# One weight load for both activation parts: 512-column products in the second layer of a hybrid encoder

## The chip, the cores and the metric

The kernel runs on one core of one Trainium2 chip. The metric is the device time of one execution in microseconds (us). TensorE (PE in the rows) multiplies, and its weight loads have rows of their own (PEld); VectorE is DVE, ScalarE is ACT, GpSimd is POOL, and SP issues most of the DMAs.

## The reference

A trunk of two layers over 272 tokens (16 meta tokens and 256 of the input), 1024 wide, all in float32:

```python
for layer in range(DEPTH):                       # DEPTH = 2
    hn = rms_norm(h, norm_mix[layer])
    proj = hn @ w_in[layer]                      # 1024 -> q, k, v, SSM input, pooling input, 3 x 1024 gates
    y_attn = windowed_gqa_attention(q, k, v, attn_sink[layer])
    y_ssm = bidirectional_s5(...)
    y_pool = multiscale_pool(...)
    ys = jnp.stack([y_attn, y_ssm, y_pool], axis=2)
    branch = jnp.einsum("blcm,cmd->blcd", ys, w_branch[layer])
    gates = jax.nn.sigmoid(proj[..., OFF_GATE:].reshape(b, L, N_BRANCH, D_MODEL))
    merged = jnp.sum(gates * branch, axis=2)
    h = h + merged @ w_out[layer]
    hn = rms_norm(h, norm_mlp[layer])
    h = h + jnp.square(jax.nn.relu(hn @ w_up[layer])) @ w_down[layer]   # 1024 -> 4096 -> 1024
return rms_norm(h, norm_final)[:, N_META:]       # the meta tokens are dropped
```

## The kernel before, in words

Channels lie on the 128 partitions and tokens along the columns. Layer 0 works on all 272 tokens; in layer 1 the meta tokens are needed only for keys, values, SSM and pooling inputs, so that all other products have `N = 256` columns (`t0 = 16` is left out).

**Products in three passes.** Every float32 operand is split in two parts, a high one rounded to `fp32r` and a low one with the remainder, and a product of two 128x128 blocks is made of three `fp32r` matmuls in `product` (line 183): high weights times high activations, high weights times low activations, low weights times high activations. All blocks of one output tile accumulate in one PSUM tile (`mm`, three buffers of one bank). Each matmul has a weight load of its own, so that the high block is loaded twice.

**Weights.** A chunk is eight 128x128 blocks. `need` (line 160) issues its DMA three chunks ahead, and two chunks ahead splits it: ACT writes `hi` (line 169) and DVE writes `lo` (line 170). Both engines run their instructions in the order in which they stand.

**Out of PSUM.** A gate (`gate`, line 1049) is multiplied by the norm's scale on DVE (L1055), and ACT takes a tanh of it. A branch product (`branch`, line 1059) is multiplied by the gate on DVE (L1076, or L1073 in the first branch) and added to `acc` (L1077). A product of the MLP's first matrix (`up`) goes through three ACT instructions (L1166 to L1168) and one of DVE (L1169), one of its second matrix (`dn`) through two of DVE (L1185, L1186). Queries are copied by ACT (L988) for a rotation on PE (`swq`).

**Order.** The main stream of products goes through SSM inputs (`pju`), keys, values, queries (`pjk`, `pjv`, `pjq`), pooling inputs (`pjp`), gates and branches (`pjg`, `br`), the SSM's output gate (`gl`), the merge (`wo`), and twice sixteen `up` chunks and sixteen `dn` chunks. Attention, SSM scans, pooling and the preparation of the SSM's operands are side work: generators that `pump` steps between half chunks of the main stream. A scheduler then orders each engine's instructions.

Of the kernel before, what the change touches and what calls it, by code (L numbers as in the profile page):

```python
# [10 lines left out]
F32 = mybir.dt.float32  # L11
# [7 lines left out]
P = 128  # L19
# [13 lines left out]
# how the side work is woven into the main stream of products: its rate per slot,  # L33
# by generator and layer, and the slots between a step and the product that uses it
# [23 lines left out]
AHEAD = 3  # chunks of weights loaded ahead of their use  # L58
SPLIT = 2  # and split
WARM = 5  # products that warm the tensor engine up  # L60
# [4 lines left out]
# polynomials, highest power first: e^r on +-ln(2)/2, sine and cosine on +-pi/4  # L65
# [5 lines left out]
# columns of the constant table  # L71
# [3 lines left out]
# columns of the SSM operands of eight groups  # L75
# [9 lines left out]
def encoder(ctx: ExitStack, tc: tile.TileContext, a: dict, out: bass.AP):  # L85
# [5 lines left out]
    class TE:  # L91
        """The tensor engine; side work does not overtake what is written before it."""
# [18 lines left out]
    h = cp.tile([P, KT, NT], F32, name="h")  # L111
    xh = cp.tile([P, KT, NT], F32, name="xh")
    xl = cp.tile([P, KT, NT], F32, name="xl")
# [43 lines left out]
    WHOLE = {(0, 0), (0, 2)}  # (layer, branch) multiplied in float32 without a split  # L157
# [21 lines left out]
    def first_need(k):  # L179
        """The first chunks, split one by one."""  # L180
        need(k - SPLIT, pinned=True)

    def product(ps, ws, xs, start=True, stop=True):
        n = len(ws)
        for i, ((wh, wl), (xa, xb)) in enumerate(zip(ws, xs)):
            TE.matmul(ps, _r(wh), _r(xa), start=start and i == 0, stop=False)
            TE.matmul(ps, _r(wh), _r(xb), start=False, stop=False)
            TE.matmul(ps, _r(wl), _r(xa), start=False, stop=stop and i == n - 1)

    ORDER = ((0, 1, 2, 3), (2, 3, 0, 1))  # SSM quarters; the last operands made are still on chip  # L190
# [28 lines left out]
    side = []  # L219

    class Side:
        """Steps of a generator, each yielding its cost and the slots it has to wait after it;
        a slot of the main stream allows it `rate`."""
# [24 lines left out]
    def pump(boost=0.0):  # L248
        """Side work for one slot of the main stream."""
        for e in list(side):  # L250
            e.run(boost or e.rate)
# [20 lines left out]
    def feed(n, k, t0):  # L272
        """Scaled, split copy of h's k-th block, and its squares; the last are returned apart."""
        hk = h[:, k, t0:]
        S.activation(_r(xh[:, k, t0:]), hk, AF.Copy, scale=gain(n, k))
        V.scalar_tensor_tensor(  # L276
            _r(xl[:, k, t0:]), hk, gain(n, k), xh[:, k, t0:], ALU.mult, ALU.subtract
        )
        return squares(k, t0)
# [5 lines left out]
    def stats(name, t0, parts=None):  # L285
        """1/rms of every token, on all partitions; `parts`' squares are still to be summed."""
# [28 lines left out]
    def exp_acc(x):  # L315
        """e^x for x clamped to [-170, 100], to float32's accuracy."""
# [19 lines left out]
    def twice(c, s, co, so, w):  # L336
        """Cosine and sine of twice the angle."""
        V.scalar_tensor_tensor(so, s, 2.0, c, ALU.mult, ALU.mult)
        V.scalar_tensor_tensor(w, s, -2.0, s, ALU.mult, ALU.mult)
        V.tensor_scalar(co, w, 1.0, None, ALU.add)  # L340
# [13 lines left out]
    def ssm_params(l):  # L354
# [4 lines left out]
        m5 = st(5)  # mag^4, mag^3, mag^2, mag, 1  # L359
# [49 lines left out]
        ct, sn = st(4), st(4)  # cosines and sines of 1..4 times the angle  # L409
# [12 lines left out]
        # f = (abar - 1) / lambda  # L422
# [13 lines left out]
        # the factors by half quarter and part: f's real part, and its imaginary part signed  # L436
# [3 lines left out]
        # input side: mag^(3-j) e^(-i (j+1) theta) f, rows in the order  # L440
        # (step, quarter, parity, pair), the steps from the last to the first
# [30 lines left out]
        # powers of abar on the output side  # L472
# [15 lines left out]
    def prepare(l, q, bun):  # L488
        """The SSM operands of the groups 8q..8q+7 of layer l."""
# [16 lines left out]
        # rotations by j times the chunk's angle, and the decay of a chunk  # L506
# [15 lines left out]
        # output matrices: [part, group, power, channel]; power 0 is C itself  # L522
# [17 lines left out]
        # input matrices, rows (parity, channel, step), columns (direction, state),  # L540
        # and between them the response within a chunk
# [69 lines left out]
    def prep(l):  # L611
        """Parameters and operands of layer l's SSM, ahead of the layer that uses them."""
        yield from ssm_params(l)
        for q in range(4):
            while l == 0 and q >= 2 and q - 2 not in scanned:
                yield 0.0, 1
            bun = bundle(f"b{l}{q}")
            yield from prepare(l, q, bun)
            if l == 0 or q >= 2:
                buns[l, q] = bun  # L620
            else:
                for o, e in PIECES:
                    SY.dma_start(bund[q, :, o:e], bun[:, o:e])
# [5 lines left out]
    def scan_quarter(l, q):  # L629
# [22 lines left out]
        # four runs of chunks: real part's halves, imaginary part's halves in reverse  # L652
# [8 lines left out]
        for hb in range(2):  # L661
            # no group crosses the border of a bank
# [18 lines left out]
        # states before each chunk; the chunks run backward on the last 64 partitions  # L681
# [32 lines left out]
        # rotated back, [part, group, chunk], and all chunks put in order  # L714
# [16 lines left out]
        # outputs, rows (parity, step, channel)  # L731
# [23 lines left out]
    cold = []  # quarters whose results are long out  # L755
# [9 lines left out]
    def attention(l, kr, qr, vt, waits):  # L765
# [7 lines left out]
        for gi, (q0, w, mk) in enumerate(groups):  # L773
            yps = pm.tile([P, 512], F32, tag="yps", name=f"yps{l}{gi}", bufs=1)
            n = 4 if w == P else 1
            hw = 2 * w  # columns of two heads
# [103 lines left out]
    with tc.high_priority():  # L880
# [5 lines left out]
        # the tensor engine reaches its full clock while h arrives  # L886
# [38 lines left out]
    for l in range(DEPTH):  # L925
# [3 lines left out]
        xc = [(xh[:, k, t0:], xl[:, k, t0:]) for k in range(KT)]  # L929
        if l == 0:  # L930
            rstd = None

        def scaled(o, ps):
            """Out of PSUM, with the norm's scale if it is still to come."""
# [7 lines left out]
        def proj(i, full=True, name=""):  # L942
            ps = mm_tile(f"pj{name}{l}")
            n = NT if full else N
# [6 lines left out]
        # SSM input  # L951
# [25 lines left out]
        # keys, values, queries  # L977
# [7 lines left out]
        def rope(ps, o, c0, name):  # L985
            n = NT - c0
            xe = tmp(f"xe{name}")[:, :n]
            S.activation(xe, ps, AF.Copy)  # L988
# [26 lines left out]
        def urgent(gen):  # L1015
            """Side work that starts at once, ahead of the rest."""
            e = Side(gen, 5.0, True)
            waits.append(e)
            e.step()
            e.wait += 1  # L1020
            return e
# [9 lines left out]
        # pooling input  # L1031
# [13 lines left out]
        # gates and branches  # L1045
# [3 lines left out]
        def gate(b, m):  # L1049
# [4 lines left out]
            else:  # L1054
                V.tensor_tensor(g, ps, rstd[:, t0:], ALU.mult)  # L1055
# [3 lines left out]
        def branch(b, m2):  # L1059
            ws = need(plans[l, "b", b][m2])  # L1060
            for i in range(2):
                m = 2 * m2 + i
                ps = mm_tile(f"br{l}{b}{m}")[:, :N]
                yy = [tuple(y[:, t0:] for y in ybuf(b, t)) for t in range(4)]
# [7 lines left out]
                if b == 0:  # L1072
                    V.scalar_tensor_tensor(o, g, 1.0, ps, ALU.add, ALU.mult)  # L1073
                else:
                    tb = tmp(f"gb{l}{b}{m}")[:, t0:]
                    V.scalar_tensor_tensor(tb, g, 1.0, ps, ALU.add, ALU.mult)  # L1076
# [32 lines left out]
        zx = [(zs[:, q, t0:], zs[:, 4 + q, t0:]) for q in ORDER[l]]  # L1109
        ys[2] = slots(2, f"ys{l}")  # L1110
        for m2 in range(2):
            gw = need(plans[l, "glu"][m2])
            for i in range(2):
                m = 2 * m2 + i
                ps = mm_tile(f"gl{l}{m}")[:, :N]
# [4 lines left out]
                S.activation(tb, ps, AF.Tanh, scale=0.5, bias=hb)  # L1120
# [12 lines left out]
        mgh, mgl = slots(0, f"mgh{l}"), slots(1, f"mgl{l}")  # L1133
        for m in range(8):
            hi, lo = mgh[:, m, t0:], mgl[:, m, t0:]
            S.activation(_r(hi), acc[:, m, t0:], AF.Copy, scale=0.5)
            V.scalar_tensor_tensor(_r(lo), acc[:, m, t0:], 0.5, hi, ALU.mult, ALU.subtract)
            mg.append((hi, lo))
        for m in range(8):
            ps = mm_tile(f"wo{l}{m}")[:, :N]  # L1140
            product(ps, need(plans[l, "out"][m]), mg)
            V.tensor_tensor(h[:, m, t0:], h[:, m, t0:], ps, ALU.add)
            sq7 = feed(2 * l + 1, m, t0)
        # MLP
# [3 lines left out]
        for f in range(2):  # L1148
            hid = []
            hs = [slots(i, f"hid{l}{f}{i}") for i in range(4)]  # L1150
            for m in range(16):
                ps = mm_tile(f"up{l}{f}{m}")[:, :N]
# [12 lines left out]
                hi, lo = hs[m // 8][:, m % 8, t0:], hs[2 + m // 8][:, m % 8, t0:]  # L1165
                S.activation(re, ps, AF.Relu)  # L1166
                S.activation(sq, re, AF.Square)  # L1167
                S.activation(_r(hi), re, AF.Square)  # L1168
                V.tensor_tensor(_r(lo), sq, hi, ALU.subtract)  # L1169
                hid.append((hi, lo))  # L1170
                pump()
            for m in range(8):
                ps = mm_tile(f"dn{l}{f}{m}")[:, :N]
# [11 lines left out]
                V.tensor_tensor(tb, ps, rq[:, t0:], ALU.mult)  # L1185
# [43 lines left out]
def _pack(w):  # L1229
    """[K, M] in blocks, [M/128, 128, K/128, 128]."""  # L1230
# [4 lines left out]
def _layout(i):  # L1235
# [8 lines left out]
    # SSM channels: as they enter, [quarter, parity, pair, channel], and as they leave  # L1244
    g = np.arange(512).reshape(4, 4, 2, 16)  # quarter, pair, parity, channel
# [33 lines left out]
    lam = np.stack([f["ssm_lam_re"], f["ssm_lam_im"], ld])  # i l d g n  # L1279
    o["lam"] = lam.transpose(1, 2, 4, 0, 3).reshape(L, P, 3, G)  # L1280
    # b: [l, d, g, n, q]
    b = np.stack([f["ssm_b_re"], f["ssm_b_im"]])  # c l d g n q
    b = b.reshape(2, L, 2, 4, 4, 2, 64, 16)  # c l d quarter pair b n q
    o["b_row"] = b.transpose(1, 3, 5, 7, 4, 0, 2, 6).reshape(L, 4, 2, 16, 1024)
    bc = b.reshape(2, L, 2, 4, 2, 4, 64, 16)  # c l d quarter half g n q
    o["b_col"] = bc.transpose(1, 3, 2, 6, 4, 0, 5, 7).reshape(L, 4, P, 256)
    c = np.stack([f["ssm_c_re"], f["ssm_c_im"], f["ssm_c_re"]])
    c = c.reshape(3, L, 2, 4, 8, 16, 64)  # c l d quarter g p n
# [28 lines left out]
```

## Time and profile before

| | |
|---|---|
| time, median of 3 runs | 893.82 us (893.33 to 897.0) |
| span of the profiled execution, first to last instruction | 892.9 us |
| PE busy, PEld busy | 97%, 91% of the span |
| DVE busy, ACT busy | 76%, 61% |

The page gives no time of the profiled execution beside its span of 892.9 us; the median of the runs is 0.9 us above that span. A matmul's busy time reaches from its start to the modelled end of its results, so that it overlaps with the next: what a matmul costs in a dense stream is read from start to start, or as a stretch's length over its count.

### The profile page before, as it was taken

What the parts mean: (1) busy time and instruction counts of PE and PEld (TensorE: products, weight loads), DVE (VectorE), ACT (ScalarE), POOL (GpSimd) and SP (SyncE); (2) the same over time, 40 slices, a digit from 0 to 9 for tenths busy, and PEclk for the clock granted to TensorE, in tenths of its full rate; (3) what the DMA queues carried; (4) which work ended last, traced back from release to release, by engine and by line L of the source; (5) the groups of instructions that cost most, each with busy time, mean ns of one, the idle gap of its engine ahead of it and who ended that gap; (6) DMA issues with size and microseconds to landing.
All of it is one profiled execution on the core that took longest, in us unless ns stands there. A gap on an engine that the chain in (4) does not pass through costs nothing.

```text
span 892.9 us, 18412 instructions
## 1 busy us (share of the span) xinstructions
PE 870.0 (97%) x7174; PEld 814.8 (91%) x7174; DVE 675.3 (76%) x1443; ACT 541.0 (61%) x1005; POOL 4.1 (0%) x32
## 2 busy tenths in 40 slices
PE   6999999999999999999999999999999999999995
PEld 4987777899899999999999988789999999999995
DVE  7987978899986557677896988677878755555564
ACT  5568597845567655477565467575565775357652
POOL 1000000000000000000000000000000000000000
PEclk7999999999999999999999999999999999999998
DMA  7644645454475556958766464625565565555551
GB/s 250 203 154 129 191 117 164 151 159 152 154 228 170 177 169 194 294 187 264 230 201 182 130 215 150 206 96 157 174 192 170 175 193 182 186 185 186 189 189 48
DMA packets 62520, 159.47 MB, mean 179 GB/s; under 512 B 20064, under 2 KB 25952, under 8 KB 62432
## 3 DMA queue, kind: packets, MB, share of 16 engines
q1 hardware_dynamic: 59696, 155.63, 55.8%
q10 hardware_dynamic: 2736, 2.65, 0.9%
q8 instruction: 56, 0.92, 0.4%
q14 instruction: 32, 0.26, 0.1%
HBM read 150.79 MB, written 7.47 MB: 177 GB/s over the span
## 4 chain that ended last, share of the span: by engine, by line
PE 79%; DVE 12%; ACT 4%; DMA 3%; issue 2%; DVEq 0%; ACTq 0%; SPq 0%
PE up L96 21%; PE dn L96 21%; PE pjg L96 10%; PE br L96 5%; PE wo L96 5%; DVE lo L170 3%; PE pju L96 3%; PE s L96 2%; PE pjp L96 2%; PE yps L96 1%; PE pt L101 1%; PE pjq L96 1%; PE l L96 1%; PE tp L96 1%; ACT hi L169 1%
## 5 line engine op out<-in xcount | busy, mean ns | idle before, releaser
L170 DVE TENSOR_TENSOR lo<-raw,hi 128x1024 fp32r<-128x1024 f32 x240 | 292.8, 1221 | 131.4 <-ACT hi L169 128.6
L169 ACT ACTIVATE hi<-raw 128x1024 fp32r<-128x1024 f32 x240 | 253.8, 1058 | 227.6 <-PE dn L96 75.2
L96 PE MATMUL dn<-hid,hi 128*128 128x272 f32 (+1 forms) x1024 | 188.0, 285 | 0.0
L96 PEld LDWEIGHTS dn<-hid,hi 128*128 128x128 f32 x1024 | 159.1, 188 | 0.1
L96 PE MATMUL up<-xh,hi 128*128 128x272 f32 (+1 forms) x512 | 146.2, 286 | 0.0
L96 PE MATMUL dn<-hid,lo 128*128 128x272 f32 (+1 forms) x512 | 146.1, 285 | 0.0
L96 PE MATMUL up<-xh,lo 128*128 128x272 f32 (+1 forms) x512 | 146.0, 285 | 0.0
L96 PE MATMUL up<-xl,hi 128*128 128x272 f32 (+1 forms) x512 | 145.9, 285 | 0.0
L96 PE MATMUL pjg<-xh,hi 128*128 128x272 f32 (+1 forms) x384 | 113.8, 296 | 0.0
L96 PE MATMUL pjg<-xh,lo 128*128 128x272 f32 (+1 forms) x384 | 111.2, 290 | 0.0
L96 PE MATMUL pjg<-xl,hi 128*128 128x272 f32 (+1 forms) x384 | 111.0, 289 | 0.0
L96 PEld LDWEIGHTS up<-xl,hi 128*128 128x128 f32 x512 | 96.3, 188 | 0.5 <-DVE xl L276 0.4
L96 PEld LDWEIGHTS up<-xh,hi 128*128 128x128 f32 x512 | 96.5, 189 | 0.3
L96 PEld LDWEIGHTS up<-xh,lo 128*128 128x128 f32 x512 | 96.6, 189 | 0.0
L96 PEld LDWEIGHTS dn<-hid,lo 128*128 128x128 f32 x512 | 96.5, 188 | 0.0
L96 PEld LDWEIGHTS pjg<-xh,hi 128*128 128x128 f32 x384 | 73.0, 190 | 4.9 <-issue 3.9
L96 PEld LDWEIGHTS pjg<-xh,lo 128*128 128x128 f32 x384 | 73.1, 190 | 2.1 <-issue 2.0
L96 PEld LDWEIGHTS pjg<-xl,hi 128*128 128x128 f32 x384 | 72.9, 190 | 1.8 <-issue 1.5
L96 PE MATMUL wo<-mgh,hi 128*128 128x272 f32 (+1 forms) x128 | 36.6, 287 | 0.6 <-ACT hi L169 0.6
L96 PE MATMUL wo<-mgh,lo 128*128 128x272 f32 (+1 forms) x128 | 36.2, 285 | 0.3 <-DVE lo L170 0.3
L96 PE MATMUL wo<-mgl,hi 128*128 128x272 f32 (+1 forms) x128 | 36.2, 285 | 0.1
L1167 ACT ACTIVATE rs<-re 128x272 f32<-128x272 f32 (+1 forms) x64 | 27.1, 424 | 1.8
(351 smaller groups left out, 1635.9 us busy)
## 6 DMA issues: line engine op xcount, KB each, us to landing
raw<-in_w_in_dram SPq DMA_DIRECT2D x76, 512.0 KB, 3.5
raw<-in_w_up_dram SPq DMA_DIRECT2D x64, 512.0 KB, 4.2
raw<-in_w_dn_dram SPq DMA_DIRECT2D x64, 512.0 KB, 4.0
raw<-in_w_br_dram SPq DMA_DIRECT2D x24, 512.0 KB, 4.0
raw<-in_w_out_dram SPq DMA_DIRECT2D x16, 512.0 KB, 3.7
b<-in_b_row_dram SPq DMA_DIRECT2D x16, 256.0 KB, 5.0
b<-ffd SPq DMA_DIRECT2D x16, 256.0 KB, 4.6
raw<-in_glu_w_dram SPq DMA_DIRECT2D x4, 512.0 KB, 4.3
```

Source lines behind the costliest of these rows:

```text
L96: i = nc.tensor.matmul(*args, **kw)
L101: i = nc.tensor.transpose(*args, **kw)
L169: S.activation(_r(hi), raws[j], AF.Copy)
L170: i_ = V.tensor_sub(_r(lo), raws[j], hi)
L1167: S.activation(sq, re, AF.Square)
```

## The change

In layer 1 the two parts of the activations are laid side by side: `xh` and `xl` become two halves of one tile `xx`, and the tiles of the branches' inputs, the merge and the MLP's hidden layer hold the high part of block m at place m and its low part at place m + 4, so that `both` can address the two as one operand of 2 x 256 columns. `product` then issues two matmuls for a block: high weights times both parts (512 columns, one weight load), and low weights times the high part (256 columns), which adds to the second half of the PSUM tile. `total` adds the halves on the way out: ACT copies the second half to SBUF, DVE adds the first. Layer 0, whose two parts have 544 columns, keeps its three matmuls.

```diff
-    xh = cp.tile([P, KT, NT], F32, name="xh")
-    xl = cp.tile([P, KT, NT], F32, name="xl")
+    xx = cp.tile([P, KT, 2, NT], F32, name="xx")
+    xh, xl = xx[:, :, 0], xx[:, :, 1]
...
+    def both(ap, i, t0):
+        return ap[:, i : i + 5 : 4, t0:]
...
     def product(ps, ws, xs, start=True, stop=True):
         n = len(ws)
+        if isinstance(xs[0], bass.AP):
+            c = ps.shape[1] // 2
+            for i, ((wh, wl), x) in enumerate(zip(ws, xs)):
+                TE.matmul(ps, _r(wh), _r(x), start=start and i == 0, stop=False)
+                TE.matmul(ps[:, c:], _r(wl), _r(x[:, 0]), start=False, stop=stop and i == n - 1)
+            return
...
+        side_by = 2 * N <= 512
+        xc = [xx[:, k, :, t0:] if side_by else (xh[:, k, t0:], xl[:, k, t0:]) for k in range(KT)]
+        W_ = 2 * N if side_by else N
...
+        def total(o, ps):
+            if not side_by:
+                return ps
+            S.activation(o, ps[:, N:], AF.Copy)
+            V.tensor_tensor(o, o, ps[:, :N], ALU.add)
+            return o
...
-            S.activation(xe, ps, AF.Copy)
+            if ps.shape[1] == n:
+                S.activation(xe, ps, AF.Copy)
+            else:
+                ps = total(xe, ps)
...
-                V.tensor_tensor(g, ps, rstd[:, t0:], ALU.mult)
+                V.tensor_tensor(g, total(g, ps), rstd[:, t0:], ALU.mult)
...
-                    V.scalar_tensor_tensor(o, g, 1.0, ps, ALU.add, ALU.mult)
+                    V.scalar_tensor_tensor(o, g, 1.0, total(o, ps), ALU.add, ALU.mult)
...
-                    V.scalar_tensor_tensor(tb, g, 1.0, ps, ALU.add, ALU.mult)
+                    V.scalar_tensor_tensor(tb, g, 1.0, total(tb, ps), ALU.add, ALU.mult)
...
-                S.activation(tb, ps, AF.Tanh, scale=0.5, bias=hb)
+                S.activation(tb, total(tb, ps), AF.Tanh, scale=0.5, bias=hb)
...
-            V.tensor_tensor(h[:, m, t0:], h[:, m, t0:], ps, ALU.add)
+            for c in range(0, W_, N):
+                V.tensor_tensor(h[:, m, t0:], h[:, m, t0:], ps[:, c : c + N], ALU.add)
...
-                S.activation(re, ps, AF.Relu)
-                S.activation(sq, re, AF.Square)
-                S.activation(_r(hi), re, AF.Square)
+                if side_by:
+                    total(re, ps)
+                    V.scalar_tensor_tensor(sq, re, 0.0, re, ALU.max, ALU.mult)
+                    S.activation(_r(hi), sq, AF.Copy)
+                else:
+                    S.activation(re, ps, AF.Relu)
+                    S.activation(sq, re, AF.Square)
+                    S.activation(_r(hi), re, AF.Square)
...
-                V.tensor_tensor(tb, ps, rq[:, t0:], ALU.mult)
+                V.tensor_tensor(tb, total(tb, ps), rq[:, t0:], ALU.mult)
```

On PE, at the norm's sum of squares (`ss_f`) in layer 1's first MLP half, a block of `up` stood in three rows before (`xh` and `xl` are the parts, `hi` and `lo` the weights):

```order
L96 MATMUL up_8995<-xh,hi_8919 128x256
L96 MATMUL up_8995<-xl,hi_8919 128x256
L96 MATMUL up_8995<-xh,lo_8920 128x256
L96 MATMUL ss_f_9026<-ssq,consts 128x256
L96 MATMUL ss_f_9026<-sq_8950,consts 128x256
L96 MATMUL up_9044<-xh,hi_8961 128x256
L96 MATMUL up_9044<-xl,hi_8961 128x256
L96 MATMUL up_9044<-xh,lo_8962 128x256
```

and now stands in two:

```order
L96 MATMUL up_8703<-xx,hi_8641 128x512
L96 MATMUL up_8703<-xx,lo_8642 128x256
L96 MATMUL ss_f_8726<-ssq,consts 128x256
L96 MATMUL ss_f_8726<-sq_8665,consts 128x256
L96 MATMUL up_8745<-xx,hi_8676 128x512
L96 MATMUL up_8745<-xx,lo_8677 128x256
```

The place is the same, and each block has lost one matmul with its load. So it goes for 114 chunks of layer 1, which are 912 blocks: 32 `up`, 32 `dn`, 24 gates, 12 branch, 8 `wo`, 4 query and 2 `gl` chunks. The 10 chunks of layer 1 with 272 columns and all of layer 0 keep their matmuls.

On DVE, in the last branch of layer 1 (`br` is its PSUM tile, `gb` the gated product, `lo` a chunk's low weights), one chunk took these rows before:

```order
L1076 SCALAR_TENSOR_TENSOR gb_8546<-gates_6855,br_8533 128x256
L1076 SCALAR_TENSOR_TENSOR gb_8562<-gates_6855,br_8549 128x256
L1077 TENSOR_TENSOR acc_6856<-acc_6856,gb_8546 128x256
L1077 TENSOR_TENSOR acc_6856<-acc_6856,gb_8562 128x256
L170 TENSOR_TENSOR lo_8568<-raw_8527,hi_8567 128x1024
```

and takes these now (L952 is the addition in `total`, L1104 and L1105 are the old L1076 and L1077):

```order
L952 TENSOR_TENSOR gb_8359<-gb_8359,br_8350 128x256
L952 TENSOR_TENSOR gb_8373<-gb_8373,br_8364 128x256
L1104 SCALAR_TENSOR_TENSOR gb_8359<-gates_6826,gb_8359 128x256
L1104 SCALAR_TENSOR_TENSOR gb_8373<-gates_6826,gb_8373 128x256
L1105 TENSOR_TENSOR acc_6827<-acc_6827,gb_8359 128x256
L1105 TENSOR_TENSOR acc_6827<-acc_6827,gb_8373 128x256
L170 TENSOR_TENSOR lo_8381<-raw_8344,hi_8380 128x1024
```

Two additions have come in ahead of the products that they feed, and the next low weights stand behind all six.

On ACT, among the last gates of layer 1, nothing read the PSUM tile of a gate before; now each gate and each branch product has a copy (L951) in ACT's row, between the splits of the weights (L169), the tanh (L1081) and the SSM's GELU (L761, whose input `yq` comes by DMA):

```order
L951 ACTIVATE gates_6826<-pjg_8047 128x256
L761 ACTIVATE zt<-yq_1_8007 128x272
L1118 ACTIVATE zs_7443<-zt 128x256
L169 ACTIVATE hi_8103<-raw_8075 128x1024
L1081 ACTIVATE gates_6826<-gates_6826 128x256
L951 ACTIVATE gates_6826<-pjg_8074 128x256
L951 ACTIVATE gb_8116<-br_8107 128x256
```

The row of the second copy stands behind the GELU and a split. Over the whole program DVE has 144 instructions more (each output tile that changed has one more, a tile of `up` two), ACT 36 more, and PE 912 matmuls fewer.

## Rows read from the trace of the kernel before

**Rows 1.** The page: span, and busy time of each engine.

```profile
span 892.9 us, 18412 instructions
PE 870.0 (97%) x7174; PEld 814.8 (91%) x7174; DVE 675.3 (76%) x1443; ACT 541.0 (61%) x1005; POOL 4.1 (0%) x32
```

**Rows 2.** The chain that ended last: start us, length us, what it was.

```profile
279.93 42.36 PE up L96 x336
...
528.02 0.44 PE pt L101 x4
...
705.43 0.86 PE ss_f L96 x4
...
746.04 45.44 PE dn L96 x384
791.48 45.44 PE up L96 x384
...
882.41 0.44 DVE db L1185
```

**Rows 3.** Busy time by stretch of layer 1, and the granted clock.

```profile
core 0: us, PE busy (x) PEld busy (x) DVE busy (x) ACT busy (x) POOL busy (x), PEclk, DMA share, GB/s
530.00:560.00 30.00, 30.00 (x222) 24.28 (x219) 26.37 (x63) 20.73 (x39) 0.00 (x0) 1.00 0.45 150
560.00:600.00 40.00, 38.93 (x326) 32.44 (x325) 28.72 (x72) 25.59 (x54) 0.00 (x0) 0.96 0.45 147
600.00:640.00 40.00, 40.00 (x415) 38.42 (x414) 32.93 (x61) 23.45 (x35) 0.00 (x0) 1.00 0.52 158
640.00:677.00 37.00, 36.20 (x292) 34.99 (x292) 28.26 (x51) 21.56 (x38) 0.00 (x0) 1.00 0.61 193
746.00:882.00 136.00, 136.00 (x1152) 136.00 (x1151) 76.92 (x99) 71.08 (x111) 0.00 (x0) 1.00 0.54 171
```

**Rows 4.** Two weight loads after a pause of PE, in order of time.

```profile
702.21 0.19 PEld L96 LDWEIGHTS up<-xl,hi 128*128 128x128 f32 x1 [0.23 <-DVE xl L276]
702.32 0.19 PEld L96 LDWEIGHTS up<-xh,lo 128*128 128x128 f32 x1
```

**Rows 5.** Matmuls after which PE empties before the next load, in order of time.

```profile
530.56 0.28 PE L96 MATMUL pjg<-xh,lo 128*128 128x256 f32 x1
530.77 0.20 PEld L96 LDWEIGHTS yps<-pts,vt 128*64 128x64 f32 x4
...
539.92 0.59 PE L96 MATMUL pps<-dl,raw 128*128 128x256 f32 x2
540.44 0.29 PEld L96 LDWEIGHTS s<-qk 64*128 64x128 f32 x2 [0.33 <-issue]
```

**Rows 6.** Groups (460 to 880 us): busy us, mean ns, idle before and releasers.

```profile
L169 ACT ACTIVATE hi<-raw 128x1024 fp32r<-128x1024 f32 x126 | 133.2, 1058 | 131.4 <-PE dn L96 42.8 <-PE up L96 23.0 <-issue 17.7
...
L1055 DVE TENSOR_TENSOR gates<-pjg,rstd_m 128x256 f32<-128x256 f32 x24 | 10.0, 417 | 6.4 <-PE pjg L96 6.3
...
L988 ACT ACTIVATE xeq<-pjq 128x256 f32<-128x256 f32 x4 | 1.4, 361 | 0.0
...
L749 ACT ACT_TABLE_LOAD x3 | 3.8, 1283 | 3.6 <-DMA yq<-yd 3.6
```

**Rows 7.** The chain in layer 1's last branch.

```profile
669.06 1.14 DVE lo L170
670.19 0.66 DVE gb L1076 x2
...
673.99 1.14 DVE lo L170
```

More of the change, by code (lines that the diff above doesn't have):

```diff
@@ L928, in encoder @@
         xs = [(xh[:, k, :], xl[:, k, :]) for k in range(KT)]
-        xc = [(xh[:, k, t0:], xl[:, k, t0:]) for k in range(KT)]
+        side_by = 2 * N <= 512
+        xc = [xx[:, k, :, t0:] if side_by else (xh[:, k, t0:], xl[:, k, t0:]) for k in range(KT)]
+        W_ = 2 * N if side_by else N
         if l == 0:
             rstd = None
+        def total(o, ps):
[4 more added lines that the diff above has]
+            return o
         def scaled(o, ps):
@@ L943, in proj @@
             ps = mm_tile(f"pj{name}{l}")
-            n = NT if full else N
+            n = NT if full else W_
             ws, x_ = need(i), xs if full else xc
@@ L1062, in branch @@
                 m = 2 * m2 + i
-                ps = mm_tile(f"br{l}{b}{m}")[:, :N]
-                yy = [tuple(y[:, t0:] for y in ybuf(b, t)) for t in range(4)]
+                ps = mm_tile(f"br{l}{b}{m}")[:, :W_]
+                yy = [
+                    both(ys[b], t, t0) if side_by else tuple(y[:, t0:] for y in ybuf(b, t))
+                    for t in range(4)
+                ]
                 if (l, b) in WHOLE:
@@ L1108, in encoder @@
         cold.clear()
-        zx = [(zs[:, q, t0:], zs[:, 4 + q, t0:]) for q in ORDER[l]]
+        zx = [
+            both(zs, q, t0) if side_by else (zs[:, q, t0:], zs[:, 4 + q, t0:]) for q in ORDER[l]
+        ]
         ys[2] = slots(2, f"ys{l}")
@@ L1114, in encoder @@
                 m = 2 * m2 + i
-                ps = mm_tile(f"gl{l}{m}")[:, :N]
+                ps = mm_tile(f"gl{l}{m}")[:, :W_]
                 product(ps, [gw[4 * i + q] for q in ORDER[l]], zx)
@@ L1132, in encoder @@
         mg = []
-        mgh, mgl = slots(0, f"mgh{l}"), slots(1, f"mgl{l}")
+        mgs = [slots(i, f"mg{l}{i}") for i in range(2)]
         for m in range(8):
-            hi, lo = mgh[:, m, t0:], mgl[:, m, t0:]
+            b_ = mgs[m // 4]
+            hi, lo = b_[:, m % 4, t0:], b_[:, 4 + m % 4, t0:]
             S.activation(_r(hi), acc[:, m, t0:], AF.Copy, scale=0.5)
             V.scalar_tensor_tensor(_r(lo), acc[:, m, t0:], 0.5, hi, ALU.mult, ALU.subtract)
-            mg.append((hi, lo))
+            mg.append(both(b_, m % 4, t0) if side_by else (hi, lo))
         for m in range(8):
-            ps = mm_tile(f"wo{l}{m}")[:, :N]
+            ps = mm_tile(f"wo{l}{m}")[:, :W_]
             product(ps, need(plans[l, "out"][m]), mg)
-            V.tensor_tensor(h[:, m, t0:], h[:, m, t0:], ps, ALU.add)
+            for c in range(0, W_, N):
+                V.tensor_tensor(h[:, m, t0:], h[:, m, t0:], ps[:, c : c + N], ALU.add)
             sq7 = feed(2 * l + 1, m, t0)
@@ L1151, in encoder @@
             for m in range(16):
-                ps = mm_tile(f"up{l}{f}{m}")[:, :N]
+                ps = mm_tile(f"up{l}{f}{m}")[:, :W_]
                 ws = need(plans[l, "up", f][m])
@@ L1164, in encoder @@
                 sq = tmp(f"rs{l}{f}{m}")[:, t0:]
-                hi, lo = hs[m // 8][:, m % 8, t0:], hs[2 + m // 8][:, m % 8, t0:]
-                S.activation(re, ps, AF.Relu)
-                S.activation(sq, re, AF.Square)
-                S.activation(_r(hi), re, AF.Square)
+                b_ = hs[m // 4]
+                hi, lo = b_[:, m % 4, t0:], b_[:, 4 + m % 4, t0:]
+                if side_by:
[6 more added lines that the diff above has]
+                    S.activation(_r(hi), re, AF.Square)
                 V.tensor_tensor(_r(lo), sq, hi, ALU.subtract)
-                hid.append((hi, lo))
+                hid.append(both(b_, m % 4, t0) if side_by else (hi, lo))
                 pump()
             for m in range(8):
-                ps = mm_tile(f"dn{l}{f}{m}")[:, :N]
+                ps = mm_tile(f"dn{l}{f}{m}")[:, :W_]
                 for q in range(2):
```

## The prediction

> **What bounds the kernel now.** I read the page first, then the chain, then the stretches of layer 1. PE and its weight loads are busy nearly the whole span, DVE three quarters of it [rows 1]; the busy share of PE says little, since overlapping matmuls fill it, so the chain has to say where PE decides. In the MLP it does alone: 384 matmuls follow each other in 45.44 us with nothing between them [rows 2], 0.1183 us each, and in the same stretch DVE is busy 57% and ACT 52% [rows 3]. Layer 0's are 42.36 / 336 = 0.1261 us [rows 2], with 272 columns instead of 256.
>
> Before the merge it is otherwise. From 530 to 677 us DVE is busy 116.3 of 147 us [rows 3], and in the last branch the chain runs on DVE alone: from one `lo` at 669.06 to the second next at 673.99 are two chunks, 2.47 us each [rows 7].
>
> **What a 512-column matmul costs.** This is the term on which the sign hangs, and the trace has no such row. The question is what the 0.1183 us are made of. [...]
>
> [...] A load with no matmul beside it gives way to the next one after 0.11 us [rows 4], and the transposes, each with a load of 128 columns, follow each other in 0.44 / 4 = 0.110 us [rows 2]; so a load alone doesn't set 0.118. Second, where PE has to empty before the next load, a stream can be timed without a load beside it: the float32 passes of `pps` are 0.215 us each (as those of `ss_f`, 0.86 / 4 [rows 2], half the column rate at the full clock), and the next load starts 0.52 us after the first of two, which is 0.09 after the second one's stream; after the `fp32r` matmul it starts 0.21 us after its start [rows 5], so that its stream took 0.21 - 0.09 = 0.12 us, to some 0.01, with no load running beside its end. [...]
>
> [...]
>
> [...] A block then takes 0.235 + 0.118 = 0.353 us instead of 0.355. Where PE sets the pace, in 64 chunks of `up` and `dn` and 8 of `wo`, that is 576 blocks: **-1.1 us** (-12.7 to +3 by the bounds). The loads saved themselves cost nothing now, because they lie beside the streams.
>
> **What is added, and where it lies.** A copy of a 128x256 tile out of PSUM takes ACT 0.36 us (L988), an operation of DVE on one 0.42 alone [rows 6] and 0.33 in a row, two in 0.66 [rows 7].
>
> - *MLP, inside:* 16 + 32 additions of `up` and `dn` come on DVE between 746 and 882 us, 16 of them in `dn` and two in each of 16 `up` tiles; 48 x 0.42 = 20 us on 76.9 of 136 [rows 3] leave DVE idle 39 us. Nothing, and ACT loses work there. Were this cover gone, it would cost those 20 us.
> - *Tail:* the last `dn` tile's way out is on the chain (the DVE row at 882.41 [rows 2]). Copy and addition come before it: 0.36 + 0.42 = **+0.8**.
> - *Last branch:* DVE sets the pace with 2.47 us a chunk; two additions make it 3.13, which is over the 8 x 0.353 = 2.82 us of PE. Eight additions: 8 x 0.33 = **+2.6**. The split of the next low weights stands behind them, and PE waits for that.
> - *Output gate of the SSM (`gl`):* its results go through ACT and DVE in turn before the last branch can start; one copy and one addition more on that way, **+0.8**.
> - *Gates and the first two branches:* 24 + 16 tiles, 40 additions, 13.2 us of DVE in a stretch where it has some 30 us idle in all [rows 3]. Both ends are possible: 0 if the idle time takes them, 13.2 if each stands in the way. ACT's row is new as a place to wait, too: its split of 1.06 us and the GELU, before whose table loads ACT stood still 3.6 us in all for a DMA [rows 6], now stand ahead of copies, and what is queued behind a late copy is DVE's addition, then DVE's next `lo`, then PE. Three PSUM buffers cover two chunks of that. As DVE is already busy 79% with work that comes in bursts, I take nearly a third of the upper end: **+4**. The 256 blocks here save 0.5 us by the price above, which this estimate includes.
> - *Queries:* the addition comes before the rotation for which PE waits, four times some 0.25: **+1**.
> - *Merge:* a second addition to `h` before the last part of `xx` that `up` needs: **+0.4**. Otherwise DVE's chunk of `wo` stays under PE's.
>
> The copies of ACT in `dn` and `wo` lie beside PE. SP's DMAs are the same; three pairs among them change places in the scan stretch, with nothing on the chain behind them.
>
> The sum is -1.1 + 0.8 + 2.6 + 0.8 + 4 + 1 + 0.4 = +8.5 us on the span of 892.9, 901.4; the runs' median lies 0.9 above that span, so 902 us.
>
> **Rivals.** *The load is the cost after all (faster).* If the 512 columns stream in 0.215 us beside their load, and the 256 stay at 0.118, a block takes 0.333: 576 x 0.022 = -12.7 us, and with the same costs of 9.6 the time is 891. If the 256-column matmul also falls to the 0.110 of the transposes, it takes 0.325: -17.3 us, 886, and with part of the 256 blocks of the gate stretch, less. Below 889.3 (0.5% faster) it comes when the two matmuls of a block take less than 0.3305 us together. For it speaks that loads are busy in the same rhythm as matmuls, so a trace can't wholly part the two; against it rows 5 and the two layers' difference. [...]
>
> [...]
>
> *DVE takes the additions in its idle time.* Without the terms for gates, `gl` and queries, 902.3 - 5.8 = 896.5: no change. Its 30 us of idle time speak for it; that they come in front of the very rows that wait for PE speaks against.
>
> *The way out becomes the bound.* With all 13.2 us of the gate stretch on the path, 902.3 + 9.2 = 911.5.
>
> **How the numbers follow.** The forecast (columns cost the same, the gate stretch pays in part) has 0.50; the load as the cost 0.17, at 887 as the middle of its two forms; a part of it 0.10; DVE's idle time 0.15; the way out as bound 0.08. A change of 0.5%, 4.5 us, is about what a measurement of this kernel can tell from none, and the limits are 889.3 and 898.3. Faster is nearly all of the first rival and a little of the second, 0.18; the same, the rest of these two and the third, 0.25; slower, 0.57. The forecast's own range is 898 to 906. For 8 in 10 the range has to take in the upper half of the first rival and to stop short of the last: 887 to 908.
>
> **What would show it.** Right: `up` and `dn` stretches of some 45.2 us (256 matmuls in each, a 512-column start to the next start 0.235 us); 3.1 us between the `lo` rows of the last branch; DVE and not PE on the chain from 640 to 677; the same layer 0. Wrong: MLP stretches of 42.6 us or less, which is the first rival; or DVE with idle time left in the gate stretch and no more of it on the chain. A pause of PE at the step from `up` to `dn`, where the last hidden tile now goes ACT, DVE, DVE, ACT, DVE, would add a cost that I have put at nothing.

## The result and the profile after

The changed kernel takes 906.2 to 909.5 us, 1.0158 times the kernel before (95% interval 1.0127 to 1.0189): some 15 us slower, where +8.5 had been forecast, and just over 908 us, the upper end of the stated range. The first profiled execution, at a mean granted clock of 0.71, took 1493.0 us and is left out, so the rows below are from the same kernel run again (`again`: median 908.71 us against 892.75, ratio 1.0174, 1.0159 to 1.0190).

The page, which answers to [rows 1]:

```profile
span 906.8 us, 16758 instructions
PE 870.9 (96%) x6262; PEld 771.5 (85%) x6262; DVE 726.6 (80%) x1587; ACT 548.0 (60%) x1041; POOL 4.1 (0%) x32
```

PE has lost 912 matmuls and is busy as long; DVE has 51 us more. The chain of the changed kernel, which answers to [rows 2, 7] (start us, length us, what):

```profile
592.84 5.49 PE pjg L96 x16
...
638.89 7.41 PE pjg L96 x32
...
651.21 5.60 PE pjg L96 x32
...
679.31 1.14 DVE lo L170
...
682.78 1.14 DVE lo L170
...
686.26 1.13 DVE lo L170
...
760.02 45.15 PE dn L96 x256
805.17 44.80 PE up L96 x256
...
895.22 0.39 ACT db L951
...
895.63 0.43 DVE db L952
```

The MLP does what was forecast: 45.15 and 44.80 us for 128 blocks each, 0.353 and 0.350 us a block. The two new rows of the tail are 0.39 and 0.43 us. But three groups of gate matmuls are uneven: 16 blocks take 5.60 us at 651, the same 16 take 7.41 at 639, and 8 take 5.49 at 593, twice what they need. Busy time by stretch, which answers to [rows 3], and one short stretch in it (us, busy of PE, PEld, DVE, ACT and POOL, granted clock, DMA share, GB/s):

```profile
530.00:560.00 30.00, 29.55 (x167) 21.02 (x164) 26.91 (x68) 22.15 (x46) 0.00 (x0) 1.00 0.45 151
560.00:600.00 40.00, 36.10 (x242) 27.38 (x241) 32.41 (x84) 27.11 (x60) 0.00 (x0) 0.91 0.48 160
600.00:640.00 40.00, 38.10 (x275) 31.25 (x274) 31.79 (x64) 25.66 (x46) 0.00 (x0) 0.99 0.44 139
640.00:677.00 37.00, 34.40 (x222) 29.14 (x222) 30.86 (x58) 23.34 (x48) 0.00 (x0) 0.96 0.56 176
746.00:882.00 136.00, 136.00 (x776) 118.66 (x775) 100.03 (x159) 71.21 (x116) 0.00 (x0) 1.00 0.57 187
...
592.00:598.00 6.00, 5.16 (x16) 4.39 (x17) 5.19 (x12) 3.10 (x8) 0.00 (x0) 0.50 0.28 87
```

From 592 to 598 the granted clock is 0.50, right after a pause of PE of 3.90 us. The waits of PE from 490 to 720 us (us in total, times, longest):

```profile
PE pjg L96 <- DVE gates L952: 5.8, 2, 3.9
PE wo L96 <- ACT mg L1167: 3.6, 1, 3.6
PE br L96 <- DVE ys L1157: 2.6, 2, 1.8
```

In the kernel before, the longest wait in this place was 0.9 us, and the merge (`wo`) started at 675.3:

```profile
PE yps L96 <- ACT pts L833: 0.9, 1, 0.9
```

```profile
675.28 0.68 PE L96 MATMUL wo<-mgh,hi 128*128 128x256 f32 x2
```

So the whole loss lies ahead of the MLP: the merge starts 14.6 us later than before (689.9 against 675.3), and from there to the end it is 0.7 us less.

What happens in the longest pause is seen in the timelines of PE, ACT and DVE (start us, us, engine, line, what; in brackets the idle time before and what ended it):

```profile
585.87 0.28 PE L96 MATMUL pjg<-xx,lo 128*128 128x256 f32 x1
...
588.65 0.28 PE L96 MATMUL br<-yp,lo 128*128 128x256 f32 x1
592.84 0.79 PE L96 MATMUL pjg<-xx,hi 128*128 128x512 f32 x1 [3.90 <-DVE gates L952]
...
586.07 1.06 ACT L169 ACTIVATE hi<-raw 128x1024 fp32r<-128x1024 f32 x1 [2.71 <-PE pjg L96]
587.14 1.28 ACT L819 ACT_TABLE_LOAD   x1
...
590.07 0.51 ACT L821 ACTIVATE p<-p,sc 128x272 f32<-128x272 f32 x1
590.48 0.19 ACT L821 ACTIVATION_READ_ACCUMULATOR p<-p,sc 128x1 f32 x1
590.57 0.36 ACT L951 ACTIVATE gates<-pjg 128x256 f32<-128x256 f32 x1
...
590.32 0.72 DVE L737 TENSOR_TENSOR x<-z,b10s 128x544 f32<-128x544 f32 x1
...
592.39 0.39 DVE L952 TENSOR_TENSOR gates<-gates,pjg 128x256 f32<-128x256 f32 x1
```

The last gate product is done at 586.15. Its copy (L951) stands in ACT's queue behind a weight split, a table load and the softmax (L821), and runs at 590.57; its addition (L952) stands in DVE's queue behind rows of the SSM scan (L737) and runs at 592.39. Until then the PSUM tile is taken, all three are full, and PE waits.

### The profile page after: what moved, and what is told of

Its sections match the earlier page's. It is cut to its first block, busy times and chain, and to the rows that moved or that the text cites. A ratio compares the mean times of both kernels' runs of the same rounds, so it can differ in the third digit from the quotient of the medians.

```text
span 1491.2 us, 16758 instructions
## 1 busy us (share of the span) xinstructions
PE 1468.4 (98%) x6262; PEld 1187.6 (80%) x6262; DVE 736.8 (49%) x1587; ACT 550.6 (37%) x1041; POOL 4.1 (0%) x32
## 4 chain that ended last, share of the span: by engine, by line
PE 98%; DVE 1%; ACT 1%; issue 0%; POOL 0%; DVEq 0%; ACTq 0%; POOLq 0%
PE up L96 21%; PE dn L96 20%; PE pjg L96 17%; PE br L96 9%; PE wo L96 6%; PE pjp L96 3%; PE pju L96 3%; PE pjq L96 3%; PE s L96 2%; PE l L96 2%; PE yps L96 2%; PE y L96 2%; PE pt L101 2%; PE gl L96 1%; PE tp L96 1%; PE pjv L96 1%
## 5 line engine op out<-in xcount | busy, mean ns | idle before, releaser
L169 ACT ACTIVATE hi<-raw 128x1024 fp32r<-128x1024 f32 x240 | 253.5, 1057 | 605.7 <-PE up L96 155.1
L96 PE MATMUL up<-xx,hi 128*128 128x272 f32 (+1 forms) x768 | 296.0, 461 | 0.0
L96 PE MATMUL dn<-hid,hi 128*128 128x272 f32 (+1 forms) x768 | 291.8, 455 | 0.0
L96 PE MATMUL pjg<-xx,hi 128*128 128x272 f32 (+1 forms) x576 | 246.3, 500 | 2.0 <-DVE gates L952 2.0
L96 PEld LDWEIGHTS up<-xx,hi 128*128 128x128 f32 x768 | 169.5, 234 | 44.1 <-issue 21.6
L96 PE MATMUL up<-xx,lo 128*128 128x272 f32 (+1 forms) x512 | 200.9, 392 | 0.0
L96 PEld LDWEIGHTS pjg<-xx,hi 128*128 128x128 f32 x576 | 151.4, 286 | 41.0 <-issue 22.6
L96 PE MATMUL pjg<-xx,lo 128*128 128x272 f32 (+1 forms) x384 | 163.7, 426 | 0.0
L96 PEld LDWEIGHTS up<-xx,lo 128*128 128x128 f32 x512 | 119.8, 234 | 3.0 <-issue 0.2
L96 PEld LDWEIGHTS pjg<-xx,lo 128*128 128x128 f32 x384 | 106.0, 276 | 5.9 <-issue 4.0
L96 PE MATMUL wo<-mg,hi 128*128 128x272 f32 (+1 forms) x192 | 80.8, 499 | 3.5 <-ACT mg L1167 3.5
```

Source lines behind the costliest of these rows:

```text
L96: i = nc.tensor.matmul(*args, **kw)
L169: S.activation(_r(hi), raws[j], AF.Copy)
```

## The experiments

Each time is set against runs of the kernel before on the same chip. "Over none" is the difference to the kernel before plus the 4.2 us by which `no_total` is under it, that is, the price of a way out over having none. Such a price carries the intervals of two comparisons, together some 2 us.

**The changed kernel again** (no edit).

> The changed kernel itself once more, for a profile at the full granted clock. The forecast's theory (the 512 columns cost what two matmuls of 256 cost, and the way out costs the rest): up and dn stretches of layer 1 of about 45.2 us each, as 256 matmuls in 128 blocks of 0.353 us, and the whole loss of 12 to 15 us ahead of the MLP, between 490 and 700 us of the span, with DVE or ACT on the chain of waits there. The rival that the 512-column matmul itself is dearer (0.242 us or more): up and dn stretches of 46 us or more. The rival that the load is the cost: 43 us or less, and then over 20 us lost ahead of the MLP.

It took 16.0 us more than before, a little over the 12 to 15 expected; the MLP stretches and the place of the loss are as the forecast's theory has them.

**Three matmuls again, in the new tiles.**

```diff
-                TE.matmul(ps, _r(wh), _r(x), start=start and i == 0, stop=False)
+                TE.matmul(ps[:, :c], _r(wh), _r(x[:, 0]), start=start and i == 0, stop=False)
+                TE.matmul(ps[:, c:], _r(wh), _r(x[:, 1]), start=False, stop=False)
```

> The changed kernel's tiles and its way out, but each block again in three matmuls of 256 columns, two of them with the high weights loaded apart, into the two halves of the PSUM tile. What differs from the changed kernel is the 512-column matmul alone. The forecast's theory (the way out costs, the matmul gives 0.002 us a block): about 910 us, within 3 us of the changed kernel. The rival that the 512-column matmul is what costs: back to 895 to 900 us. The rival that the load saved gives time back: 915 us or more.

907.09 us, +14.3, ratio 1.0162 (1.0145 to 1.0179): within 2 us of the changed kernel. The 512-column matmul isn't the loss.

**Two matmuls, the way out of before.** The merge's second addition and the new rows of `up` are gone too.

```diff
-            S.activation(o, ps[:, N:], AF.Copy)
-            V.tensor_tensor(o, o, ps[:, :N], ALU.add)
-            return o
+            return ps[:, :N]
...
```

> The changed kernel's two matmuls to a block, but the way out of the kernel before: results are read from the first half of the PSUM tile alone, with no copy and no second addition, so that the low-part products of layer 1 are left out of the result. The forecast's theory: the way out is gone, and the time is that of the kernel before less the 1 us of the matmuls, 891 to 895 us. The rival that the 512-column matmul is dearer: 898 us or more. The rival that the load saved gives time: 886 us or less.

888.52 us, -4.2, ratio 0.9952 (0.9937 to 0.9966). It lies between the two theories: the matmuls give more than the 1 to 2 us forecast. Its stretch with the first pause has a clock of 1.00, where the kernel before had 0.96 [rows 3] and the changed one 0.91:

```profile
560.00:600.00 40.00, 39.92 (x280) 29.50 (x281) 29.29 (x73) 28.79 (x58) 0.00 (x0) 1.00 0.50 160
```

**Matmuls by themselves.** A kernel of runs of 64 matmuls (128 for float32) with one tile name each.

> Matmuls alone; the whole computation is left out. Runs of 64 fp32r matmuls into PSUM, each with a load of 128 columns, with 64, 128, 192, 256, 272, 320, 384, 448 and 512 columns; 256 and 512 columns also with loads of 64 and of 32 columns; float32 with 128 and 256; 256 columns once more at the end. Spacing from start to start. The forecast's theory: time goes with the columns, 0.118 us at 256 (whatever the load), 0.126 at 272, 0.235 at 512. [...] The third case, that each column further costs what 256 to 272 cost: 0.242 at 512.

Its chain (`nd` 256 columns, `ne` 272, `nh` 448, `ni` 512, each with a load of 128 columns; `mpu` 256 and `mqu` 512 with a load of 64; `fl` 256 in float32, `back` as `nd`):

```profile
56.39 7.69 PE nd L106 x64
64.09 8.02 PE ne L106 x64
...
92.61 13.22 PE nh L106 x64
105.83 14.55 PE ni L106 x64
120.38 7.26 PE mpu L106 x64
...
134.89 14.71 PE mqu L106 x64
...
178.72 27.63 PE fl L106 x128
...
222.00 7.69 PE back L106 x64
```

By 64: 0.120 us at 256, 0.125 at 272, 0.207 at 448, 0.227 at 512. So 512 columns cost 1.89 times 256, less than the 0.235 forecast and more than the 0.215 of the first rival. With a load of 64 columns, 256 cost 0.113: 0.007 us hang on the load. At 512 nothing does (0.230). A float32 pass of 256 columns takes 27.63 / 128 = 0.216, which is 1.80 times the 0.120 of `fp32r`, where the forecast has half the column rate. It is one execution, with a mean granted clock of 0.949 over its 232.8 us; the 256 columns at the end take the same 7.69 us as the first.

**The additions of one stretch alone.** Relative to the kernel without them (`added` is the two-instruction way out):

```diff
...
# gates_total: gates and first two branches
-                V.tensor_tensor(g, total(g, ps), rstd[:, t0:], ALU.mult)
+                V.tensor_tensor(g, added(g, ps), rstd[:, t0:], ALU.mult)
...
-                    V.scalar_tensor_tensor(tb, g, 1.0, total(tb, ps), ALU.add, ALU.mult)
+                    V.scalar_tensor_tensor(tb, g, 1.0, (added if b < 2 else total)(tb, ps), ALU.add, ALU.mult)
...
# last_total: last branch
+                    V.scalar_tensor_tensor(tb, g, 1.0, (added if b == 2 else total)(tb, ps), ALU.add, ALU.mult)
```

> Two matmuls to a block everywhere, but the halves are added only for the gates and the first two branches; everywhere else the result is read from the first half alone, so that there the low-part products of layer 1 are left out. The forecast put this stretch at 4 us. The theory after the first runs is that this stretch is the mis-sized term, with some 10 us: the run without any addition, 888.5 us, plus 10, that is 897 to 900 us. The forecast's size: 892 to 893 us. If the loss comes only from additions everywhere together: 890 us.

901.06 us, +7.8 (ratio 1.0078, 1.0052 to 1.0103): **12.0 us over none**.

> Two matmuls to a block everywhere, but the halves are added only in the last branch; everywhere else the result is read from the first half alone, so that there the low-part products of layer 1 are left out. The forecast put this at 2.6 us, so 891 us over the 888.5 of the run without additions. The theory after the first runs is a loss of 4 to 5 us, as DVE is late there and TensorE then pauses and goes on at the lower clock: 892 to 894 us. If that pause comes from the gate stretch before it: 889 us.

893.55 us, +0.2 (ratio 0.9993, 0.9979 to 1.0007): **4.5 us over none**. Its longest wait of PE, two rows of DVE's timeline in the branch, and the stretch behind it:

```profile
PE wo L96 <- ACT mg L1170: 3.6, 1, 3.6
```

```profile
668.18 1.22 DVE L170 TENSOR_TENSOR lo<-raw,hi 128x1024 fp32r<-128x1024 f32 x1
...
671.65 1.22 DVE L170 TENSOR_TENSOR lo<-raw,hi 128x1024 fp32r<-128x1024 f32 x1
```

```profile
676.00:680.00 4.00, 4.00 (x15) 3.42 (x14) 2.71 (x7) 0.14 (x1) 0.00 (x0) 0.57 0.12 16
```

DVE works from 663.1 to 678.7 with hardly a gap; from `lo` to `lo` it needs 3.47 us here, for a split and seven operations, one of them left over from the tile before. PE waits 3.6 us for the merge's input and then has a clock of 0.57 for 4 us: (1 - 0.57) x 4 = 1.7 us, an estimate, on top of the 2.6 for eight additions.

**Halves of the way out.** Relative to the changed kernel; `copy_only` also leaves out the merge's second addition, which `add_only` keeps:

```diff
# copy_only
-            S.activation(o, ps[:, N:], AF.Copy)
-            V.tensor_tensor(o, o, ps[:, :N], ALU.add)
+            S.activation(o, ps[:, :N], AF.Copy)
...
# add_only
-            S.activation(o, ps[:, N:], AF.Copy)
-            V.tensor_tensor(o, o, ps[:, :N], ALU.add)
+            V.tensor_tensor(o, consts[:, :N], ps[:, :N], ALU.add)
```

> Half of the way out: ACT copies the first half out of PSUM, DVE adds nothing, so that the low-part products of layer 1 are left out. Theory A, the cost is DVE's time: 889 to 892 us, near the run without a way out (888.5). Theory B, the cost is that every result first waits in ACT's queue: 900 us or more. If both count: 894 to 898 us.

> The other half of the way out: DVE adds a constant table to the first half, ACT copies nothing; the second half of the products of layer 1 is left out but for the merge, and the constant changes the result. Theory A, the cost is DVE's time: 903 to 908 us, near the changed kernel (908.7). Theory B, the cost is ACT's queue: 893 us or less. If both count: 897 to 901 us.

Copy alone: 892.01 us, -1.3, so 2.9 over none. Addition alone: 896.47 us, +3.2 (ratio 1.0026, 1.0010 to 1.0043), 7.4 over none. Theory A fits the first run and not the second, and theory B fits neither. Together the halves should make 10.3, and the changed kernel has 20.2. Some 10 us belong to the pair.

**What the pair does.** Four kernels, relative to the changed one:

```diff
# act_both: t is a tile of 512 columns
...
+            S.activation(t, ps, AF.Copy)
+            V.tensor_tensor(o, t[:, N:], t[:, :N], ALU.add)
# both_apart: nobody reads spare
...
+            S.activation(spare, ps[:, N:], AF.Copy)
+            V.tensor_tensor(o, consts[:, :N], ps[:, :N], ALU.add)
# copy_then_add
+            S.activation(o, ps[:, :N], AF.Copy)
+            V.tensor_tensor(o, o, consts[:, :N], ALU.add)
# add_then_copy: for gates and branches o is a tile of its own
...
+            V.tensor_tensor(o, consts[:, :N], ps[:, :N], ALU.add)
+            S.activation(spare, o, AF.Copy)
```

> The changed kernel, but ACT copies both halves (512 columns, one instruction) into SBUF, and DVE adds them there. DVE's and TensorE's work is the same, ACT's is more by some 0.3 us a tile; a PSUM tile is free when ACT has passed. Theory H (the tile is held until two engines have come by one after the other): faster than the changed kernel, 900 us or less. Theory T (the time of the two engines together fills the stretch): 908 us or more, since ACT has more to do. Theory Q (DVE stands still behind ACT's copies): no better either, 906 us or more, since DVE waits for ACT as before.

905.59 us, +12.3, 16.5 over none: 3.7 less than the changed kernel although ACT has more to do: it is busy 127.5 of the 175 us from 530 to 705, in the changed kernel 114.8. A part of the cost may be the held tile, but less than theory H had.

> ACT copies the second half into a tile that nobody reads, and DVE adds a constant table to the first half, so that the second half of the products of layer 1 is left out but for the merge, and the constant changes the result. Both engines have the changed kernel's instructions, and both must pass before a PSUM tile is free, but DVE never waits for ACT. Theory T (engine time): 906 us or more, as the changed kernel. Theory Q (DVE's wait for ACT's copy): 899 us or less, near the run with the addition alone (896.5). Theory H (the tile is held until both have come by): in between, 899 to 905 us, since the two come by in either order, but the later one still counts.

909.30 us, +16.0, 20.2 over none, the same as the changed kernel. By its expectation theory T would be right and Q fallen; but its waits of DVE (520 to 700 us) show that the edit did not do what it was for:

```profile
DVE gb L955 <- ACT spare L954: 2.7, 1, 2.7
...
DVE gates L955 <- ACT spare L954: 2.2, 4, 1.0
```

DVE still waits for ACT's copy, five times and 4.9 us in all, though it reads nothing of it; what the two have in common is the PSUM tile. So this run decides nothing about Q.

> ACT copies the first half into SBUF, and DVE adds a constant table to the copy, so that the second half of the products of layer 1 is left out but for the merge, and the constant changes the result. ACT's and DVE's instructions are as many and as long as in the changed kernel, and DVE waits for ACT's copy as there; but a PSUM tile is free as soon as ACT alone has passed. Theory H (a tile held until two engines have passed is what makes 20 us out of 3.5 and 8): 900 us or less, near the sum of the two halves of the way out, 888.5 + 3.5 + 8. Theory T (the two engines' time): 906 us or more. In between, 901 to 905 us: the hold is a part of it.

905.74 us, +12.0, 16.2 over none: 4.0 less, between what the two theories expect and near T's end. A tile that ACT alone sets free is worth some 4 us; DVE still waits for ACT, and 6 us over the two halves' 10.3 remain.

> DVE adds a constant table to the first half, and ACT then copies the sum into a tile that nobody reads, so that the second half of the products of layer 1 is left out but for the merge, and the constant changes the result. ACT's and DVE's instructions are as many and as long as in the changed kernel, but DVE alone sets a PSUM tile free, and for gates and branches DVE never waits for ACT's copy. Theory T (the two engines' time alone): 905 us or more. Theory Q (what costs is that DVE, and with it the PSUM tile, waits for its turn in ACT's queue): 900 us or less, near the addition alone (896.5) and the copy's 3.

899.17 us, +5.0 (ratio 1.0060, 1.0038 to 1.0081), **9.3 over none**, where copy and addition apart make 10.3. Both engines have as many instructions as in the changed kernel, and ACT is busy longer, 84.3 us from 560 to 677 against 76.1; the order ACT, then DVE, is gone, and with it ACT's reading of the PSUM tile. Theory T falls, Q holds: the 10 us of the pair are DVE, and with it the PSUM tile, waiting for a place in ACT's queue. The run takes away DVE's wait and the second engine on the tile together, so it does not part Q from H. Its clock in the stretches of [rows 3]:

```profile
560.00:600.00 40.00, 39.71 (x279) 29.60 (x279) 33.60 (x85) 30.42 (x67) 0.00 (x0) 1.00 0.47 157
600.00:640.00 40.00, 38.75 (x314) 32.49 (x312) 35.65 (x70) 27.74 (x48) 0.00 (x0) 1.00 0.50 158
640.00:677.00 37.00, 34.28 (x187) 29.78 (x186) 31.90 (x66) 26.11 (x53) 0.00 (x0) 0.95 0.55 175
```

No wait of PE on a gate's way out is left in this run, and the clock stays at 1.00 from 560 to 640.

**Side by side in the MLP alone.** Everything ahead of `up` as in the kernel before; in the second kernel the last `dn` tile takes three matmuls too:

```diff
...
# mlp_only: queries, gates, br, gl and wo
+        xc_old, W_old = [(xh[:, k, t0:], xl[:, k, t0:]) for k in range(KT)], N
...
# mlp_no_tail
+                last = side_by and f == 1 and m == 7
+                ps = mm_tile(f"dn{l}{f}{m}")[:, : N if last else W_]
...
```

> Side by side only in up and dn of layer 1; queries, gates, branches, gl and the merge keep three matmuls and the way out of the kernel before. The four MLP stretches of 45.5 us become 45.0 by the traces so far, -2.0 us, and the last tile's copy and addition cost 0.8: 1 us less than the kernel before, 892 us. If the additions in the MLP cost something that the traces have not shown: 894 us or more.

> As side by side in up and dn alone, but the very last dn tile takes three matmuls and the way out of the kernel before, so that nothing is added on the way to the end. By the traces so far 2 us less than the kernel before, 891 us; if the last tile's way out was not on the path, the same as side by side in up and dn alone.

891.59 us, -1.7 (ratio 0.9988, 0.9975 to 1.0002), and 890.99 us, -2.3 (0.9980, 0.9963 to 0.9997). Both are as expected; the second is the only kernel with the whole result that is faster than the one before by more than its interval, and by a quarter of a per cent.

## Why the prediction was right in direction and wrong in size

The terms of the sum, as forecast and as measured:

| term | forecast us | measured us |
|---|---|---|
| matmuls (with the 0.5 inside the gate term) | -1.6 | -4.2 (`no_total`) |
| gates and first two branches (without that 0.5) | +4.5 | +12.0 (`gates_total`) |
| last branch | +2.6 | +4.5 (`last_total`) |
| `gl`, queries, merge, tail | +3.0 | +3.7 (the remainder, not measured) |
| sum | +8.5 | +16.0 |

The remainder supposes that the parts add up, which no run shows.

**What a 512-column matmul costs: right in size.** In the MLP a 512-column matmul's start and the next lie 0.233 us apart (median of 511 pairs) where 0.235 was forecast, and the stretches are 45.15 and 44.80 us for 45.2. No run shows the 0.235 us behind the -1.1 of the sum, nor the bounds of -12.7 and +3 beside it; what the runs show for 512 columns is 0.227 us in `columns` and 0.233 in the kernel. The rival that makes the load the cost falls: by it a block would take 0.333 us or less, and it takes 0.351. The forecast's reasoning was only partly right: it let the loads cost nothing, and in `columns` 0.007 of the 0.120 us at 256 columns hang on the load (that a part of it is the load's had 0.10), while 512 columns alone cost 0.227. Why they cost 0.233 in the kernel stays open. The matmul term came out 2.6 us better all the same. By the stretches ([rows 2] against 45.15 and 44.80) the blocks give 0.3 and 0.6 us per stretch, some 2 us in all four; the rest lies in the gate stretch, where the kernel before in its profiled execution lost 40 x 0.04 = 1.6 us of clock [rows 3] and `no_total` lost none.

**Gates and the first two branches: the step that failed.** The forecast saw the row of ACT, the splits and table loads in front of a copy, and the chain of addition, `lo` and PE behind it. It then priced the additions as time of DVE, took nearly a third of 13.2 us, and let three PSUM buffers cover the rest. The addition alone is not far from that price: 7.4 us over none in the whole of layer 1, where the forecast's terms sum to 10.1. What was not priced is that copy and addition stand in series in two queues, each full of other work, and that the PSUM tile is held through both. In the whole of layer 1 that is some 10 us, the difference of `add_then_copy` and the changed kernel being 10.9; in the profiled executions the merge starts at 681.0 and 689.9 us, so 8.9 of it lie ahead of the merge. No run changes the order in the gate stretch alone; what `gates_total` shows of it is 12.0 us where 4.5 was forecast.

**The pause is paid twice.** This was not in the sum either. Behind its long waits PE ran at the lower clock, 0.50 from 592 to 598 us: by the rows above, 40 x 0.09 + 40 x 0.01 + 37 x 0.04 = 5.5 us of clock between 560 and 677 us, against 1.6 in the kernel before and none in `no_total`. It is an upper figure, since PE also waits in those stretches, and it is a part of the 12.0, not beside it. Behind the pause before `wo` come 23 x 0.07 = 1.6 us, a part of the 4.5:

```profile
677.00:700.00 23.00, 19.02 (x98) 15.86 (x97) 20.48 (x45) 12.78 (x26) 0.00 (x0) 0.93 0.37 120
```

The row to read it from was there: clock 0.96 from 560 to 600 [rows 3]. But the clock is not the whole loss. `three_mm` has the whole way out, and its profiled execution shows 1.00 from 560 to 677; it still took 904.5 us:

```profile
560.00:677.00 117.00, 111.16 (x1007) 102.27 (x1006) 99.59 (x216) 79.27 (x160) 0.00 (x0) 1.00 0.50 161
```

Nor does the clock fall behind long pauses alone. In `mlp_only`, where PE waits 1.6 us at most from 560 to 600, the profiled execution lost 40 x 0.13 = 5.2 us of clock there; it took 897.3 us, where the median of that kernel is 891.6:

```profile
560.00:600.00 40.00, 38.40 (x301) 32.34 (x301) 26.93 (x69) 22.50 (x48) 0.00 (x0) 0.87 0.40 133
```

In the changed kernel the stretch at 0.50 lies right behind the 3.90 us pause; what brings the lower clock on, these runs do not show.

**Last branch: right mechanism, one part left out.** DVE sets the pace as forecast, and eight additions are 2.6 us; the clock after the pause before `wo` adds some 1.7, which makes 4.3 of the 4.5 measured. With some 2 us of uncertainty on the 4.5, the times alone would not tell it from 2.6; the rows do.

Of the signs named ahead, DVE is on the chain in the last branch, which now lies at 675 to 689 us, and there is no pause of PE from `up` to `dn`. But from 640 to 667 us it is PE that is on the chain, and the `lo` rows lie 3.5 us apart and not 3.1 (679.31, 682.78 and 686.26 above), with the operation left over from the tile before. Half of a sign of being wrong came too: DVE was busy 95.1 of the 117 us from 560 to 677, so it had idle time left; but its share of the chain rose from 12% to 16%.

**`gl`, queries, merge and tail** are left with 3.7 for 3.0, and the tail's two rows came to 0.82 for 0.8. **Inside the MLP** nothing was lost, as forecast: DVE's busy time rose from 76.9 to 100.0 of 136 us beside a PE without a pause.

**The rivals.** "The way out becomes the bound" (911.5 us) came nearest in size, with 12.0 of its 13.2 us, but for another reason: it has every addition's time on the path, and the additions alone cost 7.4 in the whole of layer 1. It had got the smallest chance, because the additions were weighed against 30 us of idle time of DVE. Here idle time in total did not tell what the additions cost, since they stood in a fixed order behind another engine's work.

What stays open: how the 10 us divide between the held tile and DVE's own waits. `copy_then_add` puts 4.0 on the tile, and the remaining 6 were not measured apart from the clock. By the rows from 560 to 677 us the changed kernel lost 5.5 us of clock and `add_then_copy` 37 x 0.05 = 1.9, so in the profiled executions up to 3.6 of the 10.9 between them are clock.

## What to carry to other kernels

A way out of PSUM that needs two engines one after the other can cost more than the two operations: the tile is held from the end of the product to the end of the second one, through both queues (6.6 us for the gate product above, 586.15 to 592.78), so look in the timeline at what stands in each queue ahead of it, not at idle time. Here the way out cost 20 us, and 9 with as many instructions but without that order. And price a pause of TensorE with the clock behind it: here 0.50 for 6 us behind one of 3.90.

## What the hardware showed that was not expected

- 512 columns cost less per column than 448: 0.227 / 512 = 0.444 ns against 0.207 / 448 = 0.461, each with a load of 128 columns.
- At 256 columns a smaller load shortens the matmul's spacing from 0.120 to 0.113 us, at 512 it doesn't (0.227 and 0.230): the load's share shows only at the shorter matmul.
- In `both_apart` an addition on DVE waits for a copy on ACT that reads other columns of the same PSUM tile: five waits of 4.9 us in all.
